# Moving the operands of one decoder block's matmuls to other byte offsets modulo 128

## The chip, the cores and the metric

The kernel runs on one NeuronCore of one Trainium2 chip. The metric is the time of one execution in device microseconds (us). The kernel before took 1974.78 us, the median of two runs (1974.39 and 1975.16).

## The reference

The reference is one hybrid decoder block for 256 tokens of width 2048, in float32. `proj = h @ w_in`, with `h` the rms-normalised input, gives the queries, keys, values and gates of two token mixers; both outputs are gated, merged and projected, and a gated feed-forward layer of width 5632 follows:

```
h = _rms_norm(x, attn_norm[l]);  proj = h @ w_in[l]
o_a = _nsa_mixer(...)            # compressed + selected + windowed attention
o_b = _gdn_mixer(...)            # short convolution, gated delta rule in chunks
mix = sigmoid(m_a) * (o_a @ w_branch_a[l]) + sigmoid(m_b) * (o_b @ w_branch_b[l])
x = x + mix @ w_out[l]
h2 = _rms_norm(x, ffn_norm[l])
x = x + (silu(h2 @ w_gate[l]) * (h2 @ w_up[l])) @ w_down[l]
```

Nearly all of the arithmetic is in the products with the large weight matrices, which are read once each from device memory.

## The kernel before

Every float32 number that enters a large product is split in two parts of the type fp32r, `hi` and `lo`, and a product is three matmuls: hi by hi, hi by lo and lo by hi. The matmul instruction of TensorE has a stationary operand (`lhsT`, 128 columns, which a weight load brings into the array ahead of the matmul) and a moving operand (`rhs`, which is streamed through it). In this kernel every matmul has a weight load of its own, also where the same stationary tile is used twice in a row.

`load_pair` (line 99) brings two k-tiles of a weight matrix, 128 rows by 512 columns each, into the tile `raw` by one DMA from the SP queue. ScalarE writes `whi` from it (line 107) and VectorE writes `wlo` (line 108). Both are tiles of two rows of 512 numbers to a partition, row j for k-tile j, and have three buffers each.

`chunk_tok` (line 113) makes 512 columns of a product for both tiles of 128 tokens: for each k-tile and each of the two token tiles three matmuls (lines 122 to 124), with a weight piece of 512 columns as the moving operand and a 128 by 128 piece of a transposed activation as the stationary one. `chunk_feat` (line 130) makes the same product transposed, for the convolved q, k and v of the gated delta rule: there a 128 by 128 piece of the weights is stationary and the activation, 256 tokens, is moving (lines 141 to 143).

The activations lie in tiles `hi` and `lo` with 16 k-tiles of 256 numbers to a partition. `big_tile` (line 93) takes them from a pool of four buffers of 16384 bytes, one behind the other. In the order of the program these tiles are the stationary operands of `chunk_tok`:

- `hT` (the normalised input), for `w_in`: the attention's projections, the output gates of the delta rule and the merge gates, 2112 matmuls. The same tiles are the moving operand of `chunk_feat`, 2304 matmuls.
- `oTA` and `oTB` (the outputs of the two mixers), for `w_branch_a` and `w_branch_b`, 384 matmuls each.
- `mixT`, for `w_out`, 384 matmuls.
- `h2T`, for `w_gate` and `w_up`, 2112 matmuls.
- `act`, for `w_down`, 1056 matmuls in four chunks. Its 44 k-tiles are split over three pairs of tiles: `act00` and `act10` (hi and lo of k-tiles 0 to 15, from the pool of four), `act01` and `act11` (16 to 31) and `act02` and `act12` (32 to 43), these four from another pool.

The address of a tile within a partition is fixed when the program is built. In the built program of the kernel before, `raw`, `whi`, `wlo` and every buffer of the pool of four start at 96 bytes modulo 128, and `act01`, `act11`, `act02` and `act12` start at 0. A k-tile takes 1024 bytes, a token tile 512, a row of `whi` or `wlo` 2048, so every piece that a matmul reads starts where its tile does, modulo 128.

The smaller work of the two mixers runs as side tasks between the pieces of the chunks (`run` and `pump`, lines 163 and 150): normalisations, transposes and small matmuls. A scheduler sets the final order on each engine when the program is built.

Of the kernel before, what the change touches and what calls it, by code (L numbers as in the profile page):

```python
# [9 lines left out]
F32 = mybir.dt.float32  # L10
F32R = mybir.dt.float32r
# [5 lines left out]
P = 128  # L17
S = 256
NT = 2
D = 2048  # L20
KD = D // P
# [22 lines left out]
def tile_hybrid_block(  # L44
# [22 lines left out]
    nc = tc.nc  # L67
    x = x[0]
# [11 lines left out]
    stream = ctx.enter_context(tc.tile_pool(name="stream", bufs=4))  # L80
    big = ctx.enter_context(tc.tile_pool(name="big", bufs=4))
# [1 line left out]
    psm = ctx.enter_context(tc.tile_pool(name="psm", bufs=4, space=bass.MemoryType.PSUM))  # L83
    pss = ctx.enter_context(tc.tile_pool(name="pss", bufs=4, space=bass.MemoryType.PSUM))

# [1 line left out]
    uid = [0]  # L87

    def nm(s):
        uid[0] += 1  # L90
        return f"{s}_{uid[0]}"

    def big_tile(name, dt=F32):
        return big.tile([P, KD, S], dt, tag="big", name=nm(name))

    def sps():
        return pss.tile([P, 512], F32, tag="sd", name=nm("sd"))
# [1 line left out]
    def load_pair(w, k0, c0, width):  # L99
        raw = stream.tile([P, 2, 512], F32, tag="raw", name=nm("raw"))  # L100
        nc.sync.dma_start(
            raw[:, :, :width],
            w[k0 * P : (k0 + 2) * P, c0 : c0 + width].rearrange("(k p) c -> p k c", p=P),
        )
        hi = stream.tile([P, 2, 512], F32R, tag="whi", name=nm("whi"), bufs=3)
        lo = stream.tile([P, 2, 512], F32R, tag="wlo", name=nm("wlo"), bufs=3)
        nc.scalar.activation(hi[:, :, :width], raw[:, :, :width], AF.Copy)  # L107
        nc.vector.tensor_tensor(  # L108
            lo[:, :, :width], raw[:, :, :width], hi[:, :, :width].bitcast(F32), ALU.subtract
        )  # L110
        return hi, lo

    def chunk_tok(w, c0, width, kts, stat, evac):
        ps = [psm.tile([P, 512], F32, tag="mm", name=nm("mm")) for _ in range(NT)]
        for k0 in range(0, kts, 2):
            hi, lo = load_pair(w, k0, c0, width)
            for j in range(2):
                kt = k0 + j
                for t in range(NT):
                    sh, sl = stat(kt, t)  # L120
                    o = ps[t][:, :width]
                    nc.tensor.matmul(o, lhsT=sh, rhs=hi[:, j, :width], start=kt == 0, stop=False)  # L122
                    nc.tensor.matmul(o, lhsT=sh, rhs=lo[:, j, :width], start=False, stop=False)  # L123
                    nc.tensor.matmul(o, lhsT=sl, rhs=hi[:, j, :width], start=False, stop=kt == kts - 1)  # L124
            yield
        for t in range(NT):
            evac(t, ps[t])
        yield
# [19 lines left out]
    side = deque()  # L148
# [16 lines left out]
            pump(n)  # L165

    def run_pair(ga, gb, n):
        """two chunks of which the last four k-tiles wait for the side tasks"""
        for g in (ga, gb):
            for _ in range(6):  # L170
                next(g)
                pump(n)
        drain()
# [3 lines left out]
        nc.vector.tensor_tensor(dst_lo, src, dst_hi.bitcast(F32), ALU.subtract)  # L177

    def transpose_hilo(src4, hi, lo, k0, t):
        """src4: four [P, P] pieces of a token-major tile, to k-tiles k0..k0+3 of hi and lo."""  # L180
        pt = sps()
        for i, s4 in enumerate(src4):
            nc.tensor.transpose(pt[:, i * P : (i + 1) * P], s4, ident)  # L183
        pv = pt.rearrange("p (k c) -> p k c", k=4)
        ts = slice(t * P, (t + 1) * P)
        hilo(hi[:, k0 : k0 + 4, ts], lo[:, k0 : k0 + 4, ts], pv)

# [1 line left out]
    ident = consts.tile([P, P], F32, name="ident")  # L189
    make_identity(nc, ident)  # L190
    identb = consts.tile([P, P], BF16, name="identb")
# [37 lines left out]
        nc.vector.tensor_copy(dst, pt[:, :n])  # L229
        return dst  # L230

# [1 line left out]
    scr = tc.tile_pool(name="nsa", bufs=1)  # L233
    nsa = scr.__enter__()
    hT_hi = big_tile("hT_hi", F32R)
    hT_lo = big_tile("hT_lo", F32R)
    xin = big.tile([P, NT, D], F32, tag="big", name="xin")
    for t in range(NT):
        for c in range(2):
            cs = slice(c * 1024, (c + 1) * 1024)  # L240
# [41 lines left out]
        ts = slice(t * P, (t + 1) * P)  # L282
        return hT_hi[:, kt, ts], hT_lo[:, kt, ts]

# [1 line left out]
    gates = consts.tile([P, NT, 48], F32, name="gates")  # L286
    beta = consts.tile([P, NT, H], F32, name="beta")
    gdec = consts.tile([P, NT, H], F32, name="gdec")
# [4 lines left out]
    def narrow():  # L293
# [5 lines left out]
        for k0 in range(0, KD, 8):  # L299
# [4 lines left out]
            for j in range(8):  # L304
                kt = k0 + j
                o = ps[:80, :S]
# [13 lines left out]
        nc.scalar.activation(beta, pv[:, :, 16:32], AF.Sigmoid)  # L320
        yield
        nc.vector.tensor_tensor(gdec, pv[:, :, 0:16], dtb.unsqueeze(1).to_broadcast([P, NT, H]), ALU.add)
        # softplus(a) = max(a, 0) + log1p(exp(-|a|)), the log1p as 2 artanh(e / (2 + e))
        e = consts.tile([P, NT, H], F32, name="sp_e")
        d = consts.tile([P, NT, H], F32, name="sp_d")
        s2 = consts.tile([P, NT, H], F32, name="sp_s2")
# [3 lines left out]
        nc.vector.reciprocal(d, d)  # L330
        nc.vector.tensor_tensor(e, e, d, ALU.mult)
        nc.vector.tensor_tensor(s2, e, e, ALU.mult)
        # the argument is at most 1/3, so terms to s^15 reach float32
        nc.vector.tensor_scalar(d, s2, 1.0 / 15, 1.0 / 13, ALU.mult, ALU.add)
        for q in (11, 9, 7, 5, 3):
            nc.vector.tensor_tensor(d, d, s2, ALU.mult)
# [20 lines left out]
        nc.sync.dma_start(grow_d, grow)  # L357
        yield

# [1 line left out]
    oTA_hi = big_tile("oTA_hi", F32R)  # L361
    oTA_lo = big_tile("oTA_lo", F32R)

# [21 lines left out]
        nc.vector.scalar_tensor_tensor(lo, src, gcol, hi.bitcast(F32), ALU.mult, ALU.subtract)  # L385

    def normed_T(pst, hi, lo, gcol):
        """rms-norm of four heads side by side, transposed, times a gain by channel"""
        sq = nsa.tile([P, 512], F32, tag="sq", name=nm("sq"), bufs=1)
        nc.scalar.activation(sq, pst, AF.Square)  # L390
        ss = nsa.tile([P, 4], F32, tag="ss", name=nm("ss"), bufs=4)
        nc.vector.tensor_reduce(ss, sq.rearrange("p (g d) -> p g d", g=4), AX.X, ALU.add)
        rs = nsa.tile([P, 4], F32, tag="rs", name=nm("rs"), bufs=4)
        rstd_of(ss, 1.0 / DH, EPS, rs)
        nv = nsa.tile([P, 512], F32, tag="nv", name=nm("nv"), bufs=2)
        nc.vector.tensor_tensor(
            nv.rearrange("p (g d) -> p g d", g=4),
            pst.rearrange("p (g d) -> p g d", g=4),
            rs.unsqueeze(2).to_broadcast([P, 4, P]),
            ALU.mult,  # L400
        )
        pt = sps()
        for i in range(4):
            nc.tensor.transpose(pt[:, i * P : (i + 1) * P], nv[:, i * P : (i + 1) * P], ident)
        gained(hi, lo, pt.rearrange("p (g d) -> p g d", g=4), gcol)
# [89 lines left out]
        return f  # L495

    def win_pair(pw):
        """columns 0:128 and 144:272 of a piece 272 wide, as [P, 2, 128]"""
        return bass.AP(tensor=pw.tensor, offset=pw.offset, ap=[list(pw.ap[0]), [144, 2], [1, 128]])

    def attend(gi, t, qh, ql):
# [93 lines left out]
    for gi in range(4):  # L595
        run(chunk_tok(w_in, C_Q + gi * 512, 512, KD, stat_h, evac_q(gi)), 1)

    # merge-gate logits and the product of branch A wait in DRAM for the merge
    keep = {n: dram.tile([NT, P, D], F32, name=n, bufs=1) for n in ("mA_d", "mB_d", "brA_d")}

    def evac_keep(n, c):
# [24 lines left out]
    for g in br:  # L626
        run(g)

# [1 line left out]
    oTB_hi = big_tile("oTB_hi", F32R)  # L630
    oTB_lo = big_tile("oTB_lo", F32R)
    scr = tc.tile_pool(name="gdn", bufs=1)
# [10 lines left out]
        return cw[r // 96][:, r % 96 : r % 96 + 1]  # L643

    def conv_silu(st, ps, base, silu_out):
        """short causal convolution of four heads by channel, then silu"""
        ca = gdn.tile([P, 4, S], F32, tag="ca", name=nm("ca"), bufs=2)
        for s in range(4):
            src = ps[s // 2][:, (s % 2) * S : (s % 2 + 1) * S]
            a = ca[:, s, :]  # L650
            nc.scalar.activation(a, src, AF.Copy, scale=conv_col(3, base + s))
            for i in (2, 1, 0):
                sh = 3 - i
                nc.vector.scalar_tensor_tensor(
                    a[:, sh:], src[:, : S - sh], conv_col(i, base + s), a[:, sh:], ALU.mult, ALU.add
                )
        silu_out(ca)
# [16 lines left out]
    nc.gpsimd.memset(p1, 0.0)  # L674
    p2 = gdn.tile([P, 8, 64], F32, name="p2")
    nc.gpsimd.memset(p2, 0.0)
    # one-hot columns for the blocks' inverses: lane = 32 * column group + problem
    unit = gdn.tile([P, 8, 32], F32, name="unit")
    nc.gpsimd.memset(unit, 0.0)
    uf = unit.rearrange("p c i -> p (c i)")  # L680
    for cg in range(4):
        for c in range(8):
            o = c * 32 + 8 * cg + c
            nc.gpsimd.memset(uf[cg * 32 : cg * 32 + 32, o : o + 1], 1.0)

    def gdn_prep(st, hg):
        """what hangs on the decay alone"""
        hs = slice(hg * 4, hg * 4 + 4)
        st.N = gdn.tile([P, 8, P], F32, tag="N", name=nm("N"), bufs=2)
        st.Q = gdn.tile([P, 8, P], F32, tag="Q", name=nm("Q"), bufs=2)  # L690
# [12 lines left out]
        for t in range(NT):  # L703
            for h in range(4):
                i = t * 4 + h
# [34 lines left out]
    def gdn_q(st, hg):  # L740
# [3 lines left out]
        for t in range(NT):  # L744
            for h0 in (0, 2):
                pk = sps()
                for h in (h0, h0 + 1):
                    nc.tensor.matmul(  # L748
                        pk[:, (h - h0) * 256 : (h - h0 + 1) * 256],
                        lhsT=st.kq[:, h, t, 0, :],  # L750
# [9 lines left out]
                    )  # L760
                    nc.vector.tensor_tensor(st.Q[:, i, :], pk[:, o + P : o + 2 * P], st.Q[:, i, :], ALU.mult)
                yield
        # the 32 x 32 blocks on the diagonal, a problem and eight of its columns to a lane
        ld = dram.tile([32, 32, 32], F32, tag="ld", name=nm("ld"))
        for b in range(4):
            bs = slice(32 * b, 32 * b + 32)
# [206 lines left out]
    for c in (2, 3):  # L973
        chunk_m("mB_d", c, 2)

# [1 line left out]
    mixT_hi = big_tile("mixT_hi", F32R)  # L977
    mixT_lo = big_tile("mixT_lo", F32R)

# [46 lines left out]
    for c in range(4):  # L1026
        run(chunk_tok(w_out, c * 512, 512, KD, stat_of(mixT_hi, mixT_lo), evac_out(c)))

# [1 line left out]
    act = [[], []]  # L1030
    for q in range(2):
        for i in range(3):
            if i == 2:
                act[q].append(fin.tile([P, 12, S], F32R, name=f"act{q}{i}"))
            elif i == 1:
                act[q].append(fin.tile([P, 16, S], F32R, name=f"act{q}{i}"))
            else:
                act[q].append(big_tile(f"act{q}{i}", F32R))
    rs2 = fin.tile([P, NT], F32, name="rs2")
    sst = fin.tile([P, NT], F32, name="sst")  # L1040
    nc.vector.tensor_reduce(sst, ss2, AX.X, ALU.add)
# [74 lines left out]
```

## Time and profile before

| what | value |
|---|---|
| median of two runs | 1974.78 us (1974.39 to 1975.16) |
| span of the profiled execution, first to last instruction | 1971.1 us |
| TensorE matmuls, busy | 1946.4 us (99%), 10485 records |
| TensorE weight loads, busy | 1651.0 us (84%) |
| VectorE, ScalarE, GpSimd busy | 1155.0, 928.4, 54.1 us |
| DMA | 367.04 MB, mean 186 GB/s |

The median stands 3.7 us above the span of the profiled execution; that is what lies around the span. The busy time of TensorE cannot tell how fast it works: matmuls are pipelined, a matmul of 512 columns is recorded as about 390 ns long, and the next one starts long before its end. What counts is the spacing, from the start of one matmul to the start of the next. It is read from the starts in a timeline, or from a stretch's length and its number of matmuls.

### The profile page before, as it was taken

To read this page: it belongs to the slowest core of one execution; us is meant where nothing else is said; L and a number is where in the kernel's file an instruction comes from. 1 tells how busy PE (TensorE), PEld (TensorE's weight loads), DVE (VectorE), ACT (ScalarE), POOL (GpSimd) and SP (SyncE) were. 2 spreads that over 40 slices of the span, in tenths; PEclk is the share of its full clock that TensorE was granted. 3 is DMA by queue.
4 is the path that set the end of the run, shared out by engine and by line. 5 is a ranking of instruction groups with operands and counts; after the bars stand their busy time and mean duration, and the time that the engine had idled before them with its cause. 6 is when DMAs were issued, how large, how long until landed. Compare 5 with 4: busy or idle time off the path is not lost.

```text
span 1971.1 us, 27260 instructions
## 1 busy us (share of the span) xinstructions
PE 1946.4 (99%) x10485; PEld 1651.0 (84%) x10485; DVE 1155.0 (59%) x1715; ACT 928.4 (47%) x1377; POOL 54.1 (3%) x97
## 2 busy tenths in 40 slices
PE   8999999999999999999999999999999999999999
PEld 6878877876998998999987788888888888888887
DVE  5555766655468587687774665554455444544443
ACT  5434555555454554654543544444444444443333
POOL 0001000001000000100100000000000000000000
PEclk9999999999999999999999999999999999999999
DMA  8566545546767566566574965666666666656663
GB/s 231 170 183 193 161 129 162 170 149 200 217 173 203 169 178 198 158 193 166 153 200 157 333 201 183 191 192 183 191 191 186 191 191 191 191 185 201 201 202 130
DMA packets 207605, 367.04 MB, mean 186 GB/s; under 512 B 25473, under 2 KB 34546, under 8 KB 207090
## 3 DMA queue, kind: packets, MB, share of 16 engines
q1 hardware_dynamic: 207442, 365.28, 62.1%
q8 instruction: 82, 1.34, 0.3%
q14 instruction: 49, 0.40, 0.1%
q10 hardware_dynamic: 32, 0.01, 0.0%
HBM read 355.76 MB, written 9.45 MB: 185 GB/s over the span
## 4 chain that ended last, share of the span: by engine, by line
PE 96%; DMA 2%; DVE 1%; ACT 0%; SPq 0%; issue 0%; POOL 0%; ACTq 0%; POOLq 0%; DVEq 0%
PE mm L123 25%; PE mm L124 24%; PE mm L122 24%; PE mm L141 4%; PE mm L143 4%; PE mm L142 4%; PE sd L183 1%; PE sd L668 1%; PE sd L448 1%; PE sd L561 1%; DMA Q<-grow_d 1%; PE sd L748 1%; DMA raw<-in_w_branch_b_dram 1%; PE sd L567 1%; PE sd L568 0%; PE sd L267 0%
## 5 line engine op out<-in xcount | busy, mean ns | idle before, releaser
L108 DVE TENSOR_TENSOR wlo<-raw,whi 128x1024 fp32r<-128x1024 f32 x632 | 773.7, 1225 | 658.5 <-ACT whi L107 656.1
L107 ACT ACTIVATE whi<-raw 128x1024 fp32r<-128x1024 f32 x632 | 669.7, 1060 | 804.5 <-PE mm L124 674.4
L123 PE MATMUL mm<-wlo,hT_hi 128*128 128x512 f32 x704 | 276.7, 393 | 0.0
L124 PE MATMUL mm<-whi,hT_lo 128*128 128x512 f32 x704 | 276.5, 393 | 0.0
L124 PE MATMUL mm<-whi,h2T_lo 128*128 128x512 f32 x704 | 274.0, 389 | 0.0
L123 PE MATMUL mm<-wlo,h2T_hi 128*128 128x512 f32 x704 | 273.9, 389 | 0.0
L122 PE MATMUL mm<-whi,hT_hi 128*128 128x512 f32 x704 | 260.2, 393 | 0.0
L122 PE MATMUL mm<-whi,h2T_hi 128*128 128x512 f32 x704 | 249.9, 390 | 0.0
L143 PE MATMUL mm<-hT_hi,wlo 128*128 128x256 f32 x768 | 218.4, 285 | 0.0
L141 PE MATMUL mm<-hT_hi,whi 128*128 128x256 f32 x768 | 218.4, 285 | 0.0
L142 PE MATMUL mm<-hT_lo,whi 128*128 128x256 f32 x768 | 218.3, 284 | 0.0
L124 PEld LDWEIGHTS mm<-whi,hT_lo 128*128 128x128 f32 x704 | 132.3, 188 | 27.7 <-issue 1.1
L123 PEld LDWEIGHTS mm<-wlo,hT_hi 128*128 128x128 f32 x704 | 132.3, 188 | 27.5 <-issue 1.1
L124 PEld LDWEIGHTS mm<-whi,h2T_lo 128*128 128x128 f32 x704 | 132.2, 188 | 27.5
L122 PEld LDWEIGHTS mm<-whi,h2T_hi 128*128 128x128 f32 x704 | 132.2, 188 | 27.1
L123 PEld LDWEIGHTS mm<-wlo,h2T_hi 128*128 128x128 f32 x704 | 132.2, 188 | 27.0
L122 PEld LDWEIGHTS mm<-whi,hT_hi 128*128 128x128 f32 x704 | 132.1, 188 | 26.3 <-issue 0.2
L141 PEld LDWEIGHTS mm<-hT_hi,whi 128*128 128x128 f32 x768 | 147.2, 192 | 0.6
L142 PEld LDWEIGHTS mm<-hT_lo,whi 128*128 128x128 f32 x768 | 147.2, 192 | 0.2
L143 PEld LDWEIGHTS mm<-hT_hi,wlo 128*128 128x128 f32 x768 | 146.9, 192 | 0.4
L123 PE MATMUL mm<-wlo,act 128*128 128x512 f32 x352 | 138.5, 393 | 0.0
L124 PE MATMUL mm<-whi,act 128*128 128x512 f32 x352 | 138.4, 393 | 0.0
(288 smaller groups left out, 2247.7 us busy)
## 6 DMA issues: line engine op xcount, KB each, us to landing
raw<-in_w_in_dram SPq DMA_DIRECT2D x272, 512.0 KB, 3.7
raw<-in_w_gate_dram SPq DMA_DIRECT2D x88, 512.0 KB, 4.4
raw<-in_w_up_dram SPq DMA_DIRECT2D x88, 512.0 KB, 3.7
raw<-in_w_down_dram SPq DMA_DIRECT2D x88, 512.0 KB, 4.7
raw<-in_w_branch_a_dram SPq DMA_DIRECT2D x32, 512.0 KB, 4.7
raw<-in_w_branch_b_dram SPq DMA_DIRECT2D x32, 512.0 KB, 4.9
raw<-in_w_out_dram SPq DMA_DIRECT2D x32, 512.0 KB, 4.7
wc<-in_w_cmp_dram SPq DMA_DIRECT2D x16, 256.0 KB, 4.2
```

The costliest lines, as they stand in the source:

```text
L107: nc.scalar.activation(hi[:, :, :width], raw[:, :, :width], AF.Copy)
L108: nc.vector.tensor_tensor(lo[:, :, :width], raw[:, :, :width], hi[:, :, :width].bitcast(F32), ALU.subtract)
L122: nc.tensor.matmul(o, lhsT=sh, rhs=hi[:, j, :width], start=kt == 0, stop=False)
L123: nc.tensor.matmul(o, lhsT=sh, rhs=lo[:, j, :width], start=False, stop=False)
L124: nc.tensor.matmul(o, lhsT=sl, rhs=hi[:, j, :width], start=False, stop=kt == kts - 1)
L141: nc.tensor.matmul(o, lhsT=hi[:, j, ws], rhs=xh[:, kt, :], start=first, stop=False, skip_group_check=True)
L142: nc.tensor.matmul(o, lhsT=hi[:, j, ws], rhs=xl[:, kt, :], start=False, stop=False, skip_group_check=True)
L143: nc.tensor.matmul(o, lhsT=lo[:, j, ws], rhs=xh[:, kt, :], start=False, stop=last, skip_group_check=True)
L183: nc.tensor.transpose(pt[:, i * P : (i + 1) * P], s4, ident)
L448: nc.tensor.matmul(pc[:60, :P], lhsT=kp[:, l0 + l, :], rhs=wc[:, l, :], start=l0 + l == 0, stop=l0 + l == 31)
L561: nc.tensor.transpose(pt[:n, r * P : (r + 1) * P], pb[:, r, c0 : c0 + n], ident)
L567: nc.tensor.matmul(po, lhsT=wh, rhs=ph[:n], start=i == 0, stop=False)
```

## The change

It moves tiles by a few bytes and leaves the work as it is. The built programs, before and changed, hold the same instructions in the same order on every engine; what differs is the addresses, and that ScalarE and VectorE write `whi` as two rows of 512 with a gap between them instead of 1024 numbers on end.

- `big_tile` and `xin` take 8 numbers (32 bytes) more, so the four buffers of the pool start at 96, 0, 32 and 64 modulo 128.
- `whi` gets 8 numbers between its two rows, so row 0 starts at 96 and row 1 at 0. `wlo` stays at 96 in both rows. To tell the rows apart, the three matmuls of `chunk_tok` stand twice in the source, for j = 0 and j = 1.
- The four later `act` tiles get 32 numbers more and start at chosen offsets inside. The act tiles have new names: `actAa` and `actAb` are hi and lo of the first 16 k-tiles, `actBa` and `actBb` of the next 16, `actCa` and `actCb` of the last 12.

Offsets modulo 128 of what a matmul reads, before and changed (`whi` is 96 before, and 96 in row 0 and 0 in row 1 changed; `wlo` is 96 in both):

| activation | hi before, changed | lo before, changed |
|---|---|---|
| hT | 96, 64 | 96, 32 |
| oTA, oTB | 96, 0 | 96, 96 |
| mixT | 96, 64 | 96, 32 |
| h2T | 96, 0 | 96, 96 |
| act, k-tiles 0 to 15 | 96, 64 | 96, 32 |
| act, k-tiles 16 to 31 | 0, 112 | 0, 16 |
| act, k-tiles 32 to 43 | 0, 96 | 0, 80 |

The diff, without comments that were removed:

```diff
     def big_tile(name, dt=F32):
-        return big.tile([P, KD, S], dt, tag="big", name=nm(name))
+        b = big.tile([P, KD * S + 8], dt, tag="big", name=nm(name))
+        return b[:, : KD * S].rearrange("p (k s) -> p k s", k=KD)
...
-        hi = stream.tile([P, 2, 512], F32R, tag="whi", name=nm("whi"), bufs=3)
+        hi = stream.tile([P, 2, 528], F32R, tag="whi", name=nm("whi"), bufs=3)
+        hi = hi.rearrange("p j c -> p (j c)")[:, :1040].rearrange("p (j c) -> p j c", j=2)[:, :, :512]
...
-                    nc.tensor.matmul(o, lhsT=sh, rhs=hi[:, j, :width], start=kt == 0, stop=False)
-                    nc.tensor.matmul(o, lhsT=sh, rhs=lo[:, j, :width], start=False, stop=False)
-                    nc.tensor.matmul(o, lhsT=sl, rhs=hi[:, j, :width], start=False, stop=kt == kts - 1)
+                    if j == 0:
+                        nc.tensor.matmul(o, lhsT=sh, rhs=hi[:, 0, :width], start=kt == 0, stop=False)
+                        nc.tensor.matmul(o, lhsT=sh, rhs=lo[:, 0, :width], start=False, stop=False)
+                        nc.tensor.matmul(o, lhsT=sl, rhs=hi[:, 0, :width], start=False, stop=False)
+                    else:
+                        nc.tensor.matmul(o, lhsT=sh, rhs=hi[:, 1, :width], start=False, stop=False)
+                        nc.tensor.matmul(o, lhsT=sh, rhs=lo[:, 1, :width], start=False, stop=False)
+                        nc.tensor.matmul(o, lhsT=sl, rhs=hi[:, 1, :width], start=False, stop=kt == kts - 1)
...
-    xin = big.tile([P, NT, D], F32, tag="big", name="xin")
+    xin = big.tile([P, KD * S + 8], F32, tag="big", name="xin")[:, : NT * D].rearrange("p (t d) -> p t d", t=NT)
...
+    OFF = ((28, 24), (4, 20))
     act = [[], []]
     for q in range(2):
         for i in range(3):
-            if i == 2:
-                act[q].append(fin.tile([P, 12, S], F32R, name=f"act{q}{i}"))
-            elif i == 1:
-                act[q].append(fin.tile([P, 16, S], F32R, name=f"act{q}{i}"))
+            if i > 0:
+                n = (16, 12)[i - 1]
+                a = fin.tile([P, n * S + 32], F32R, name=("actB", "actC")[i - 1] + "ab"[q])
+                off = OFF[q][i - 1]
+                act[q].append(a[:, off : off + n * S].rearrange("p (k s) -> p k s", k=n))
             else:
-                act[q].append(big_tile(f"act{q}{i}", F32R))
+                act[q].append(big_tile("actA" + "ab"[q], F32R))
```

## Rows read from the trace of the kernel before

**Rows 1.** The page: engines' busy time, share and records; the chain by engine.

```profile
PE 1946.4 (99%) x10485; PEld 1651.0 (84%) x10485; DVE 1155.0 (59%) x1715; ACT 928.4 (47%) x1377; POOL 54.1 (3%) x97
...
PE 96%; DMA 2%; DVE 1%; ACT 0%; SPq 0%; issue 0%; POOL 0%; ACTq 0%; POOLq 0%; DVEq 0%
```

**Rows 2.** Windows of TensorE: stretch, length, busy (records under way), clock, DMA.

```profile
518.80:555.10 36.30, 36.30 (x305) 1.00 0.71 198
592.90:636.40 43.50, 43.50 (x194) 1.00 0.69 198
1327.50:1371.00 43.50, 43.50 (x194) 1.00 0.63 185
1844.60:1866.30 21.70, 21.70 (x97) 1.00 0.69 217
1866.40:1888.70 22.30, 22.30 (x97) 1.00 0.58 189
1888.80:1905.50 16.70, 16.70 (x73) 1.00 0.61 187
```

**Rows 3.** Timeline of TensorE, h2T: start, us, engine, line, out<-moving,stationary.

```profile
1500.07 0.39 PE L123 MATMUL mm<-wlo,h2T_hi 128*128 128x512 f32 x1
...
1502.79 0.39 PE L123 MATMUL mm<-wlo,h2T_hi 128*128 128x512 f32 x1
```

**Rows 4.** Timeline of TensorE, act, k-tiles 16 to 31.

```profile
1867.98 0.40 PE L123 MATMUL mm<-wlo,act 128*128 128x512 f32 x1
1868.21 0.40 PE L124 MATMUL mm<-whi,act 128*128 128x512 f32 x1
1868.45 0.40 PE L122 MATMUL mm<-whi,act 128*128 128x512 f32 x1
...
1870.08 0.40 PE L123 MATMUL mm<-wlo,act 128*128 128x512 f32 x1
```

**Rows 5.** Timeline of TensorE, hT, behind a pause.

```profile
174.64 0.40 PE L124 MATMUL mm<-whi,hT_lo 128*128 128x512 f32 x1
174.87 0.40 PE L122 MATMUL mm<-whi,hT_hi 128*128 128x512 f32 x1
175.11 0.39 PE L123 MATMUL mm<-wlo,hT_hi 128*128 128x512 f32 x1
175.33 0.39 PE L124 MATMUL mm<-whi,hT_lo 128*128 128x512 f32 x1
175.56 0.40 PE L122 MATMUL mm<-whi,hT_hi 128*128 128x512 f32 x1
...
176.72 0.39 PE L124 MATMUL mm<-whi,hT_lo 128*128 128x512 f32 x1
```

**Rows 6.** Timeline of TensorE, the feature stage, behind a pause.

```profile
585.09 0.28 PE L142 MATMUL mm<-hT_lo,whi 128*128 128x256 f32 x1
...
586.16 0.28 PE L142 MATMUL mm<-hT_lo,whi 128*128 128x256 f32 x1
```

**Rows 7.** The chain in order of time: start, us, engine, line, records.

```profile
579.26 3.46 PE sd L748 x16
```

**Rows 8.** Groups by line: instruction, shape, count, busy and mean ns, idle before.

```profile
L108 DVE TENSOR_TENSOR wlo<-raw,whi 128x1024 fp32r<-128x1024 f32 x632 | 773.7, 1225 | 658.5 <-ACT whi L107 656.1
L107 ACT ACTIVATE whi<-raw 128x1024 fp32r<-128x1024 f32 x632 | 669.7, 1060 | 804.5 <-PE mm L124 674.4 <-PE mm L142 73.3 <-issue 31.1
```

**Rows 9.** Waits of TensorE for the split weights: total us, times, longest.

```profile
PE mm L123 <- DVE wlo L108: 3.3, 4, 1.7
PE mm L122 <- ACT whi L107: 1.0, 2, 0.7
```

## The prediction

> **What bounds the kernel now.** I read the page first: engines and chain [rows 1]. The reader is to see that matmuls are busy for 99% of the span and make up 96% of the chain of work that ended last. The other engines are busy for 59% and less. Only the speed of TensorE can move this time, and the engine is never short of work, so I looked for the spacing of its matmuls, from start to start.
>
> The windows give it by stage [rows 2]. Each of the six stretches holds large matmuls alone, and a window also counts the records under way when it opens: two of 512 columns (390 ns long, started some 227 ns apart), two or three of 256. So the first row says 36.30 us over 302 or 303 matmuls of 256 columns, 120 ns each; the second and third 43.50 us over 192 of 512 columns, 226.6 ns; the fourth, with `act` of k-tiles 0 to 15, 21.70 us over 95 or 96, 226 to 228. The last two, `act` of the later k-tiles, give 22.30 us over 95 or 96 and 16.70 us over 71 or 72: 232 to 235. [...]
>
> The timelines make it sharper. With `h2T` stationary, 12 spacings take 1502.79 - 1500.07 = 2.72 us, 226.7 ns each [rows 3]. With `act` of k-tiles 16 to 31, 9 spacings take 2.10 us, 233.3 each [rows 4]. The instructions are the same, and so are the moving tiles, which start at 96 modulo 128 in both. The stationary tiles start at 96 in the first case and at 0 in the second. That is the only trace of an offset's cost in this kernel: equal offsets 226.7, unequal ones 6.6 ns more.
>
> **The change, part by part.** No instruction is added, taken away or moved, on any engine or queue. What can change is how long each takes.
>
> *Writing whi in two rows.* ScalarE takes 1060 ns for a `whi`, VectorE 1225 ns for a `wlo` [rows 8]. One of each serves 12 matmuls, 12 x 226.7 = 2720 ns, or 24 of 256 columns, 24 x 120 = 2880 ns. So each engine works less than half of the time that it has, three buffers lie between, and TensorE waited 4.3 us in all for these two lines [rows 9]. I put this at nothing; the cover is gone only if one of them took over twice as long. Should matmuls become faster, the weights must come faster too: 193 GB/s at 226.7 ns (524288 bytes in 2.72 us) would be 202 at 216 ns, and the fourth window moved 217 [rows 2].
>
> *Matmuls whose weight load lies at another offset.* A weight load runs while the matmul before it streams, so the pair that counts is a matmul's moving piece and the next stationary one. The price of an unequal pair at the new distances stands in no row, so I bound it. Above: 233.3 ns, the settled spacing at the one unequal distance in this trace [rows 4]. Below: 216 ns, the shortest spacing at which records with a 128-column load before each follow one another here, the float32 products of line 748, 3.46 us over 16 [rows 7]. Between the two lies what equal offsets do behind a pause, when the load and the stream are not yet in step: 9 spacings in 176.72 - 174.64 = 2.08 us, 231.1 ns each, some 0.22 and some 0.24 us long, before they settle at 226.7 [rows 5]. I read these as samples of many relative positions of load and stream, and take 231 for an unequal pair, nearest to the settled unequal row and 4.4 above the equal one.
>
> - `hT`, `mixT` and `act` of k-tiles 0 to 15 (hi at 64, lo at 32, against 96 and 0): every pair is unequal. 2112 + 384 + 384 = 2880 matmuls x 4.4 ns = 12.7 us.
> - `h2T`, `oTA`, `oTB` (hi at 0, lo at 96): only row 0 of `whi` with hi is unequal, one pair in three, and these stand close together, in the six matmuls of row 0; the six of row 1 are equal. Since nine matmuls behind a pause are still unsettled [rows 5], six do not suffice to fall back into step. Ends: one third of 2880 (4.2 us) and all (12.7 us); I take two thirds, 8.4 us.
> - The later `act`, 672 matmuls: unequal before and nearly all unequal after, 233.3 to 231: -1.5 us.
> - The feature stage, 2304 matmuls of 256 columns: all unequal now (moving 64 and 32, stationary 96 and 0). Behind a pause 9 spacings there take 586.16 - 585.09 = 1.07 us, 118.9 each [rows 6], below the settled 120. So unequal offsets may give 1 ns back (-2.5 us) or cost what they do elsewhere (4.4 ns, +10.1 us); I take 0.
>
> Sum: 12.7 + 8.4 - 1.5 + 0 = +19.6 us. The profiled span of 1971.1 becomes 1990.7, and with the 3.7 us that the median stands above the span the time is **1994 us**, 1% more.
>
> [...]
>
> **The rivals.**
>
> *Faster: equal offsets are what costs.* Load and stream start in the same place of every 128 bytes and stay in each other's way; a well-chosen distance frees the stream. For it: 226.7 stands 10.7 above the 216 of line 748, where the load costs nothing to see, so there is something to win. Against it: the one unequal stretch is the slower one, and all through the unsettled rows no spacing falls below 0.22 us. Price at 216: 2880 x 10.7 = 30.8, a third of 2880 x 10.7 = 10.3, 672 x 17.3 = 11.6, and 2304 x 10.7 = 24.7 in the feature stage, 77 us: 1897 us. If half of the pairs gain, 1936. It decides where the new stages settle below 226 ns.
>
> *Slower by over 2%: every unequal pair costs what act shows.* Its place is the reading of the stationary piece beside the stream, in all stages that were equal. Price: 2880 x 6.6 = 19.0; the same 19.0 for `h2T` and `oT`, if the unequal third keeps the rest out of step; 2304 x 6.6 = 15.2 in the feature stage: 53 us, 2028 us. For it: this is the only settled row with unequal offsets. Against it: it shows one distance out of many, and six distances are in use now. The point from which it decides is 39.5 us over these 8064 matmuls, 4.9 ns on the mean.
>
> *No effect: the change does not do what it says.* The later `act` tiles also lie elsewhere in the partition, behind the pool of four; it may be their place and not their offset that costs 6.6 ns. Then nothing moves: 1975 us. Against it: the other tiles lie far apart too, and all of those run at 226.7.
>
> **How the numbers follow.** Forecast 0.50, with its own range from 1980 (229 ns for an unequal pair, a third in `h2T`) to 2009 (all of `h2T`, and 10 us in the feature stage); no effect 0.12; slower 0.20; faster 0.18, of which the milder third stays within 2%. A change within 2%, 1935 to 2014 us, is about what a measurement cannot tell from none. Hence faster 0.13, within 2% 0.67, slower 0.20. The range runs from 1940, near the halved gain, to 2026, just short of the full loss; some 0.13 is left out below and 0.07 above.
>
> **What would show it right or wrong.** The busy shares will hardly move, so the spacing by stage decides, from windows of pure stretches or the timeline. Right: `hT`, `mixT` and the first `act` stretch at 229 to 233 ns, `h2T` between 228 and 231 and not settling at 226.7, later `act` slightly below 233, the feature stage at 119 to 122. Faster: some stage settles at 216 to 224. Slower: 233 and more in all of them, and a feature stage at 125 or above. No effect: 226.7 everywhere but in the later `act`, still 233. The two rows of `whi` now have lines of their own, so within one stage the spacings behind row 0 and row 1 must differ if the pair sets the price, and a `wlo` matmul with `h2T` lo, both at 96, should be the one nearest to 226.7. Wrong in another way: a wait for `whi` or `wlo` of more than a few us, which would mean that writing two rows costs time.

## The result: 1% slower, with two misses that cancel

The changed kernel takes 1993.43 us, the median of two runs (1992.97 and 1993.89), against 1974.78 before: 1.0091 times as long, with a 95% interval of 1.0062 to 1.0121. The forecast was 1994. The profiled execution has a span of 1992.2 us, 21.1 more than before, at a granted clock of 0.997 (0.998 before). The medians differ by 18.7 us only. In every run with both numbers, 1.7 or 1.8 us lie around the span; of the 3.7 us that I put there for the kernel before, some 2 us are therefore not that, but a profiled execution that was faster than the median.

The page of the changed kernel, engines and chain, answers to [rows 1]:

```profile
PE 1967.3 (99%) x10485; PEld 1648.4 (83%) x10485; DVE 1155.9 (58%) x1715; ACT 928.8 (47%) x1377; POOL 55.3 (3%) x97
...
PE 97%; DMA 2%; DVE 1%; ACT 0%; SPq 0%; issue 0%; POOL 0%; ACTq 0%; DVEq 0%; POOLq 0%
```

The same 10485 matmul records are busy for 20.9 us longer, and no other engine's row of the page moved by more than 2.6 us. So nearly the whole difference lies in how fast matmuls follow one another. The page's groups for the two engines that write the weights, and the waits of TensorE for them, answer to [rows 8] and [rows 9]:

```profile
L110 DVE TENSOR_TENSOR wlo<-raw,whi 128x1024 fp32r<-128x1024 f32 x632 | 774.0, 1226 | 674.0 <-ACT whi L109 671.0
L109 ACT ACTIVATE whi<-raw 128x1024 fp32r<-128x1024 f32 x632 | 670.0, 1061 | 819.1 <-PE mm L131 696.2
```
```profile
PE mm L126 <- DVE wlo L110: 2.5, 2, 1.9
PE mm L125 <- ACT whi L109: 0.9, 2, 0.7
```

Writing `whi` in two rows takes 1 ns more than the 1060 before, and TensorE waits 3.4 us where it waited 4.3. The windows of stretches with large matmuls alone answer to [rows 2]: the feature stage, `hT`, `h2T`, and the second and third part of `act`.

```profile
525.70:561.40 35.70, 35.70 (x306) 1.00 0.71 200
729.30:773.70 44.40, 44.40 (x193) 1.00 0.69 201
1611.60:1656.00 44.40, 44.40 (x194) 1.00 0.63 183
1887.60:1909.70 22.10, 22.10 (x97) 1.00 0.60 192
1909.80:1926.40 16.60, 16.60 (x73) 1.00 0.56 186
```

The granted clock is 1.00 in all five, as in [rows 2], so the clock is not what differs. With the records under way taken off (two or three of 256 columns, two of 512 in the long stretches, one or two in the short ones), these are 118 ns for 256 columns, and 232, 231, 230 to 233 and 231 to 234 for 512. The later `act` was 232 to 235 before, so it gained a little, which the sums below make sharper; the feature stage gained as well. The timeline of `h2T` answers to [rows 3]. Its lines 125 to 127 are the matmuls of the first k-tile of a pair, 129 to 131 those of the second:

```profile
1652.15 0.40 PE L126 MATMUL mm<-wlo,h2T_hi 128*128 128x512 f32 x1
1652.39 0.40 PE L127 MATMUL mm<-whi,h2T_lo 128*128 128x512 f32 x1
1652.62 0.40 PE L129 MATMUL mm<-whi,h2T_hi 128*128 128x512 f32 x1
...
1655.19 0.40 PE L127 MATMUL mm<-whi,h2T_lo 128*128 128x512 f32 x1
```

From the first to the last row are 13 spacings (one record among them stands for two matmuls), 3.04 us: 233.8 ns each, a little above the stage's mean of 232.0. Before, they were an even 226.7.

Summed from start to start over all neighbouring large matmuls of a stage, the traces give, in us:

| stage | before | changed | difference | forecast |
|---|---|---|---|---|
| hT, mixT, first act | 641.2 | 652.7 | +11.5 | +12.7 |
| h2T, oTA, oTB | 657.9 | 672.1 | +14.1 | +8.4 |
| later act | 156.5 | 155.6 | -0.9 | -1.5 |
| feature stage | 274.6 | 269.8 | -4.8 | 0 |
| sum | | | +19.9 | +19.6 |

### The profile page after: what moved, and what is told of

It is laid out like the page before. It is cut to its first block, busy times and chain, and to the rows that moved or that the text cites. A ratio compares the mean times of both kernels' runs of the same rounds, so it can differ in the third digit from the quotient of the medians.

```text
span 1992.2 us, 27260 instructions
## 1 busy us (share of the span) xinstructions
PE 1967.3 (99%) x10485; PEld 1648.4 (83%) x10485; DVE 1155.9 (58%) x1715; ACT 928.8 (47%) x1377; POOL 55.3 (3%) x97
## 4 chain that ended last, share of the span: by engine, by line
PE 97%; DMA 2%; DVE 1%; ACT 0%; SPq 0%; issue 0%; POOL 0%; ACTq 0%; DVEq 0%; POOLq 0%
PE mm L126 12%; PE mm L129 12%; PE mm L127 12%; PE mm L130 12%; PE mm L131 12%; PE mm L125 12%; PE mm L150 4%; PE mm L148 4%; PE mm L149 4%; PE sd L190 1%; PE sd L675 1%; PE sd L455 1%; PE sd L568 1%; PE sd L755 1%; PE sd L574 0%; PE sd L575 0%
## 5 line engine op out<-in xcount | busy, mean ns | idle before, releaser
L131 PEld LDWEIGHTS mm<-whi,hT_lo 128*128 128x128 f32 x352 | 66.2, 188 | 16.2 <-issue 0.8
L127 PEld LDWEIGHTS mm<-whi,h2T_lo 128*128 128x128 f32 x352 | 66.0, 188 | 16.2
```

The source lines that it names most:

```text
L127: nc.tensor.matmul(o, lhsT=sl, rhs=hi[:, 0, :width], start=False, stop=False)
L131: nc.tensor.matmul(o, lhsT=sl, rhs=hi[:, 1, :width], start=False, stop=kt == kts - 1)
```

## The experiments

In every experiment the matmuls are those of the kernel before, in number and, but for e8, in shape; what is meant to differ is the addresses alone. In e1 `whi` is also written as two rows, in e5 and e7 to e12 one or two small tiles share buffers, to make room, and in e9 to e12 this shifts the order of some small instructions. All use one edit, by which a table `MOVE` gives the numbers (of 4 bytes) by which hi and lo of an activation are moved in their buffers; the `act` tiles outside the pool take their entries in the same way. It is shown as in e2, e3, e4 and e6; the room of 32 numbers (128 bytes) is 64 in e10 and nothing in the others:

```diff
-    def big_tile(name, dt=F32):
-        return big.tile([P, KD, S], dt, tag="big", name=nm(name))
+    def big_tile(name, dt=F32, off=0):
+        b = big.tile([P, KD * S + 32], dt, tag="big", name=nm(name))
+        return b[:, off : off + KD * S].rearrange("p (k s) -> p k s", k=KD)
```

The table has the mean spacing in ns of every stage, worked out from the starts of neighbouring large matmuls (pauses, over 243 ns for 512 columns and over 137 for 256, left out; the unsettled matmuls behind them are in, which lifts `hT` and `oTA` by a ns where the stage is even). "Act 1, 2, 3" are its three parts. Times are single executions, but medians of five for e5, e9, e11 and e12; the kernel before ran beside them on the same chips, 1974.8 for e1 to e4 and between 1973.2 and 1978.9 for the others.

| run | hT | mixT | h2T | oTA | act 1, 2, 3 | feature | us |
|---|---|---|---|---|---|---|---|
| before | 227.7 | 226.9 | 226.8 | 228.0 | 226.9, 233.3, 233.3 | 119.9 | 1974.8 |
| changed | 231.6 | 231.7 | 232.0 | 231.9 | 231.2, 231.7, 231.8 | 117.7 | 1993.4 |
| e1 | 231.8 | 231.8 | 231.8 | 231.8 | 231.7, 231.9, 232.5 | 118.4 | 1995.6 |
| e2 | 232.0 | 232.2 | 231.7 | 231.8 | 232.2, 231.2, 227.3 | 117.9 | 1992.8 |
| e3 | 233.0 | 233.2 | 232.8 | 231.8 | 233.3, 233.3, 233.3 | 117.2 | 2001.2 |
| e4 | 233.3 | 233.3 | 230.6 | 231.0 | 233.3, 232.0, 226.8 | 118.3 | 1995.0 |
| e5 | 231.0 | 230.9 | 230.8 | 231.1 | 230.9, 231.0, 231.0 | 118.6 | 1992.0 |
| e6 | 233.0 | 233.1 | 233.3 | 233.3 | 233.1, 233.3, 233.3 | 121.8 | 2011.8 |
| e7 | 231.0 | 230.8 | 230.8 | 231.0 | 230.9, 231.1, 231.0 | 114.0 | 1982.6 |
| e8 | 231.0 | 230.9 | 230.8 | 231.0 | 230.9, 230.3, 231.4 | 118.3 | 1989.5 |
| e9 | 227.7 | 226.9 | 226.8 | 228.1 | 226.7, 226.7, 226.7 | 116.3 | 1964.5 |
| e10 | 232.4 | 232.3 | 231.2 | 231.3 | 233.0, 233.3, 232.3 | 119.2 | 1998.5 |
| e11 | 227.8 | 226.9 | 226.8 | 227.8 | 226.7, 226.7, 226.7 | 117.8 | 1966.2 |
| e12 | 227.8 | 226.9 | 226.8 | 227.5 | 226.7, 226.7, 226.7 | 113.8 | 1959.8 |

**e1, the rows of whi alone.** Only the second row of `whi` is moved by 32 bytes; the activations stay.

```diff
-        hi = stream.tile([P, 2, 512], F32R, tag="whi", name=nm("whi"), bufs=3)
+        hi = stream.tile([P, 2, 528], F32R, tag="whi", name=nm("whi"), bufs=3)
+        hi = hi.rearrange("p j c -> p (j c)")[:, : 2 * 520].rearrange("p (j c) -> p j c", j=2)[:, :, :512]
```

> Only whi's row 1 moves, to 0 modulo 128; all stationary activations stay at 96 (later act at 0). Pair theory (the distance between a moving piece and the next stationary one sets the price of each matmul alone): in h2T the two thirds of the row-1 matmuls whose moving piece is whi cost about 231 ns, all others 226.7, mean 228; time about 1984 us. Step theory (a stage settles at a fixed spacing only if offsets repeat from matmul to matmul; alternating offsets keep it unsettled): every pair, the equal ones too, means 231 to 232; time 1992 to 1998 us.

It took 1995.6 us, 20.8 more than before: this edit alone costs as much as the whole change. It does more than move a row, though; see e5.

**e2, the activations alone.** `whi` and `wlo` stay at 96; the activations have the changed kernel's offsets modulo 128.

```diff
+        "hT": (24, 16), "mixT": (24, 16), "actA": (24, 16),
+        "oTA": (8, 0), "oTB": (8, 0), "h2T": (8, 0), "actB": (28, 4), "actC": (24, 20),
```

> Only the stationary tiles move, to the offsets of the changed kernel (hi and lo differ); whi and wlo stay at 96 in both rows. Pair theory: in h2T wlo with lo (equal) at 226.7, the other two of three at about 232, mean 230; time about 1993 us. Step theory: no stage settles, all pairs mean 231 to 232, time 1992 to 1998 us.

1992.8 us, 18.0 more. So the two parts do not add up: either one takes the stages out of their even spacing (all but the last part of `act`, at 227.3), and the other then changes little.

**e3 and e4, one distance to a stage.** Hi and lo of a stage lie at one offset modulo 128, another one in each stage.

```diff
+        # e3
+        "hT": (24, 24), "mixT": (24, 24), "actA": (24, 24),
+        "oTA": (16, 16), "oTB": (16, 16), "h2T": (16, 16), "actB": (20, 20), "actC": (28, 28),
+        # e4
+        "hT": (8, 8), "mixT": (8, 8), "actA": (8, 8),
+        "oTA": (12, 12), "oTB": (12, 12), "h2T": (12, 12), "actB": (12, 12), "actC": (24, 24),
```

> One distance (stationary minus moving) in each stage, the same for hi and lo and both rows: 96 in hT, mixT and the first act, 64 in h2T and oT, 112 in act of k-tiles 16 to 31, 16 in the last act; feature stage 32. Pair theory: every stage at the unequal price, 231 to 233 ns, feature stage 118 to 122. Step theory: each stage settles after some ten matmuls in a short repeating pattern with a mean of its own between 224 and 236 ns; some distance may lie below 226.7.

> One distance in each stage again: 32 in hT, mixT and the first act, 48 in h2T and oT, 80 in act of k-tiles 16 to 31, 0 in the last act; feature stage 96. Pair theory: 231 to 233 ns but in the last act, 226.7. Step theory: each stage settles in a pattern of its own; hT at 32 repeats 233.3, as the later act tiles did before, and the last act, at equal offsets in the tile that cost 233.3, goes to 226.7. If it is the place of the later act tiles that costs, the last act stays at 233.3 and hT at 226.7.

2001.2 and 1995.0 us. Of the stages of 512 columns in the table, the thirteen with unequal offsets lie between 230.6 and 233.3, none below. The last part of `act` in e4 has its offsets equal to those of the weights, in the place where it ran at 233.3 before, and there it runs at 226.8. Its timeline:

```profile
1914.78 0.39 PE L137 MATMUL mm<-whi,actCb 128*128 128x512 f32 x1
...
1917.28 0.39 PE L136 MATMUL mm<-wlo,actCa 128*128 128x512 f32 x1
```

These are 11 spacings (one record between stands for two matmuls) in 2.50 us, 227 each. And `hT`, in the pool of four where it ran at 227.7, runs at 233.3 with its offset 32 bytes on. It is the offset, not the place.

**e5, all equal modulo 128.** The later `act` tiles come to 96 modulo 128 as well. The buffers of `whi` and `wlo` get 32 numbers of room, of which the feature stage uses 8 to put its distance at 32.

```diff
-        hi = stream.tile([P, 2, 512], F32R, tag="whi", name=nm("whi"), bufs=3)
+        hi = stream.tile([P, 1056], F32R, tag="whi", name=nm("whi"), bufs=3)
+        hi = hi[:, off : off + 1024].rearrange("p (j c) -> p j c", j=2)
...
+        "actB": (24, 24), "actC": (24, 24),
```

> A version that should beat both. All stationary activations of the 512-column stages and both weight tiles at 96 (distance 0 everywhere, the later act tiles too); only in the feature stage the weight tiles start 32 bytes later (distance 32). If what the runs so far showed holds by stage: 226.8 ns in every 512-column stage (672 matmuls of the later act gain 6.5 ns each, 4.4 us), feature stage 117.2 instead of 119.9 (2304 x 2.7 = 6.2 us): 1964 us against 1974.8. Rival (pair prices from before alone, feature stage not helped): 1970.

1991.98 us against 1975.9 beside it, a ratio of 1.0083 (1.0069 to 1.0097). Every stage of 512 columns is at 231, though all its offsets are equal modulo 128. The built program shows what I had overlooked: a weight buffer of 1056 numbers is 4224 bytes, 16 and a half times 256, so the three buffers of `whi` lie at 96, 224 and 96 modulo 256. The timeline of `h2T`:

```profile
1659.64 0.39 PE L138 MATMUL mm<-wlo,h2T_hi 128*128 128x512 f32 x1
...
1662.18 0.40 PE L137 MATMUL mm<-whi,h2T_hi 128*128 128x512 f32 x1
```

11 spacings (one record stands for two) in 2.54 us: 230.9 each. The title's "modulo 128" is half of what counts. In e1 and in the changed kernel `whi` has such a buffer too, and in e2 to e4 and e6 the pool of four has one (16512 bytes). So e1 does not tell the moved row from the buffers' 128 bytes, which by themselves give 231.0 here against e1's 231.8. And in the pool of four, hi and lo of e3, e4 and e6 lie 128 bytes apart modulo 256; one distance to a stage have only the second and third part of `act`, at 112 and 16 modulo 256 in e3, 80 and 0 in e4, 124 and 248 in e6.

**e6, a few bytes.** Modulo 128, distances of 4 and 8 bytes in the pool of four, 124 and 120 in the later `act`. Modulo 256, two thirds of the pairs in the pool of four are 132 and 136 apart; the last part of `act` is 8 bytes short of equal in every pair.

```diff
+        "hT": (1, 1), "mixT": (1, 1), "actA": (1, 1),
+        "oTA": (2, 2), "oTB": (2, 2), "h2T": (2, 2), "actB": (23, 23), "actC": (22, 22),
```

> Distances of a few bytes, one to a stage: 4 in hT, mixT and the first act, 8 in h2T and oT, 124 in act of k-tiles 16 to 31, 120 in the last act, 124 in the feature stage. If the price follows the exact byte distance, each stage has a level of its own unlike 226.8, 225 to 235; if only blocks of 16 or 32 bytes count, 4 and 8 behave as 0 (226.8) and 124 and 120 as 112 (233.3).

2011.8 us, the slowest of all, about 36 above the kernel before: 233.0 to 233.4 in all stages of 512 columns, and 121.8 in the feature stage, the only run that is slower there than before. The last part of `act`:

```profile
1990.27 0.40 PE L136 MATMUL mm<-wlo,actCa 128*128 128x512 f32 x1
...
1992.37 0.40 PE L136 MATMUL mm<-wlo,actCa 128*128 128x512 f32 x1
```

9 spacings (one record between stands for two matmuls) in 2.10 us, 233.3 each: 8 bytes are enough for the level of [rows 4].

**e7, another base.** As e5, with every tile 32 bytes further on, and the feature stage's weights moved by 64 bytes.

```diff
+    base = consts.tile([P, 8], F32, name="base")
+    nc.vector.memset(base, 0.0)
...
-            hi, lo = load_pair(w, k0, c0, 512)
+            hi, lo = load_pair(w, k0, c0, 512, 16)
```

> All tiles 32 bytes further on, moving and stationary at 0 modulo 128, distance 0; feature stage at distance 64. If only the distance counts, 226.8 in every 512-column stage, as at 96; if the offset itself counts, another level. Feature stage: between 116 and 118.

The stages of 512 columns repeat e5 to 0.2 ns: they do not notice a shift of everything by 32 bytes. That speaks for distances and against absolute offsets; other shifts, and a shift of the even state, were not run. The feature stage fell to 114.0, the surprise of this run, and the time to 1982.6 us. There the distances modulo 256 alternate between 64 and 192.

**e8, shorter weight loads.** The offsets of e5 in the 512-column stages, and the loads of the second and third part of `act` cut to 64 and 32 columns. It leaves out the products for the other tokens there.

```diff
-                    o = ps[t][:, :width]
+                    m = P if kts == KD or kt < 16 or kt == kts - 1 else 64 if kt < 32 else 32
+                    sh, sl, o = sh[:, :m], sl[:, :m], ps[t][:m, :width]
```

> Later act tiles at distance 0, and there the stationary pieces are cut to 64 columns (k-tiles 16 to 31) and 32 columns (32 to 42), so those products are left out for the other tokens; the moving pieces stay 512 columns. If the 10.7 ns above 216 come from the weight load being read beside the stream, they shrink with its columns: about 221 and 218 to 219 ns. If they are a fixed price of changing the stationary operand, both stay at 226.7. Feature stage at distance 16: 117 to 120.

230.3 and 231.4 ns, against 231.0 for whole loads in e5: half or a quarter of the columns changes next to nothing. But with these buffers the stages are not in their even state, so what a short load does to 226.7 was not measured. Inconclusive for that.

**e9, equal modulo 256.** Weight buffers of 4352 bytes, 17 times 256, and later `act` tiles that start at the weights' 96 modulo 256 (by a tile of 64 numbers ahead of them instead of 8). The feature stage's weights are moved by 64 bytes.

```diff
-        hi = stream.tile([P, 2, 512], F32R, tag="whi", name=nm("whi"), bufs=3)
+        hi = stream.tile([P, 1088], F32R, tag="whi", name=nm("whi"), bufs=3)
+        hi = hi[:, off : off + 1024].rearrange("p (j c) -> p j c", j=2)
...
-    ss2 = fin.tile([P, NT, 4], F32, name="ss2")
+    ss2 = fin.tile([P, 64], F32, name="ss2")[:, :8].rearrange("p (t c) -> p t c", t=NT)
```

> A version that should beat both: moving and stationary pieces at equal offsets modulo 256 in every 512-column stage (buffers of whi and wlo 4352 bytes apart, so modulo 512 they alternate by 256), later act tiles included; in the feature stage the weight pieces lie 64 bytes further on. If what has to repeat is the offset modulo 256, every 512-column stage settles at 226.8 and the feature stage at 114: 1974.8 - 4.4 (672 x 6.5 ns) - 13.6 (2304 x 5.9 ns) = 1957 us. If it has to repeat modulo 512, the 512-column stages stay at 231 as in the version with equal offsets modulo 128, and the time is about 1982 us.

1964.47 us against 1974.99 beside it, 0.9948 (0.9934 to 0.9962). All stages of 512 columns are at the even spacing, the later `act` too, and the three buffers alternate modulo 512. So equal offsets modulo 256 suffice (226.7 to 228.1 here), modulo 128 they do not (230.8 to 231.1 in e5). The feature stage, with 64 throughout, came to 116.3 and not to the 114.0 of e7, and so the time missed the 1957 that I expected.

**e10, half a turn.** Distances of 128, 64 and 192, and hi at 0, lo at 128 in `h2T`, `oTA` and `oTB`.

```diff
+        "hT": (32, 32), "mixT": (32, 32), "actA": (32, 32),
+        "oTA": (0, 32), "oTB": (0, 32), "h2T": (0, 32), "actB": (16, 16), "actC": (48, 48),
```

> Distances modulo 256 that modulo 128 are 0: 128 throughout in hT, mixT and the first act; 0 for hi and 128 for lo in h2T and oT; 64 in act of k-tiles 16 to 31 and 192 in the last act; feature stage 128. Whi and wlo as before. If a repeating pattern is what settles, hT gets one fixed spacing of its own (226.8, if only the distance modulo 128 counts; another level, if 256 does) and h2T, where hi and lo differ, does not settle and means 230 to 232. If the pair prices the matmul, h2T is a mixture of 226.8 and the level of hT, two thirds to one. Feature stage 114 to 120.

1998.5 us. Distances of 128, 64 and 192 throughout a stage give 232 to 233, the mixed stages 231. The groups of TensorE by line in `h2T`, where a record is the longer, the later the next matmul starts (389 or 390 at the 226.8 of the stage before, 392 to 397 at the 232.0 of the changed one):

```profile
L136 PE MATMUL mm<-whi,h2T_lo 128*128 128x512 f32 x704 | 279.4, 397 | 0.0
L135 PE MATMUL mm<-wlo,h2T_hi 128*128 128x512 f32 x704 | 278.7, 396 | 0.0
...
L134 PE MATMUL mm<-whi,h2T_hi 128*128 128x512 f32 x704 | 250.1, 391 | 0.0
```

A pair is again a matmul's moving piece and the next stationary one. From start to start, line 135, which makes an unequal pair, takes 232.4 ns on the mean; line 136, an equal pair right after an unequal one, 234.0; line 134, an equal pair after an equal one, 227.0. So the same distance of 0 costs 227 or 234, by what stands before it. Nine in ten of these spacings come back, within 1 ns, with every 12 matmuls, the loop over two k-tiles and two token tiles; so they do in e6's `h2T`, with spacings of 226 to 239. In the changed kernel 85% come back after 36 matmuls, the three weight buffers, and only 34% after 12. So these mixed stages run in sequences that repeat with their addresses. That alone would also fit a price for each pair; the equal pairs at 227 and 234 do not.

**e11 and e12, the feature stage.** As e9, with the feature stage's weights moved by 192 bytes, and by 64 (`whi`) and 192 (`wlo`).

```diff
-            hi, lo = load_pair(w, k0, c0, 512)
+            hi, lo = load_pair(w, k0, c0, 512, (48, 48))    # e11
+            hi, lo = load_pair(w, k0, c0, 512, (16, 48))    # e12
```

> As the version with equal offsets modulo 256, but in the feature stage both weight tiles lie 192 bytes further on instead of 64. If the feature stage's level is set by the distance modulo 128, it stays at 116.3 and the time at 1964 us; if 192 was the better part of the mixture of 64 and 192 that ran at 114.0, it goes to 113.3 to 114 and the time to 1958 us.

> The same, but in the feature stage whi lies 64 and wlo 192 bytes further on. If it was the mixture of the two, 113.3 to 114 ns and 1958 us, and the version with 192 throughout stays at 116; if not, 116 to 118 ns and 1964 us or more. If any alternation costs, as in the 512-column stages, it is slower than both uniform versions.

The feature stage came to 117.8 ns with 192 throughout, 116.3 with 64 throughout (e9) and 113.8 with both: the mixture does it, as the second expectation had it. e11 took 1966.16 us (ratio 0.9954, 0.9942 to 0.9967), e12 1959.75 (0.9921, 0.9908 to 0.9935), with 1975.91 for the kernel before beside both. e12 is the fastest version found. Its page:

```profile
span 1955.8 us, 27261 instructions
...
PE 1930.8 (99%) x10485; PEld 1639.8 (84%) x10485; DVE 1153.8 (59%) x1715; ACT 928.1 (47%) x1377; POOL 54.2 (3%) x97
```

Its windows of the feature stage, `h2T` and the second part of `act`:

```profile
520.30:554.80 34.50, 34.50 (x306) 1.00 0.74 204
1627.70:1671.20 43.50, 43.50 (x194) 1.00 0.65 185
1853.30:1875.00 21.70, 21.70 (x97) 1.00 0.61 192
```

and its timeline in the feature stage and in the second part of `act`:

```profile
524.74 0.28 PE L155 MATMUL mm<-hT_hi,whi 128*128 128x256 f32 x1
...
525.99 0.28 PE L157 MATMUL mm<-hT_hi,wlo 128*128 128x256 f32 x1
```
```profile
1859.64 0.39 PE L137 MATMUL mm<-wlo,actBa 128*128 128x512 f32 x1
...
1862.36 0.39 PE L137 MATMUL mm<-wlo,actBa 128*128 128x512 f32 x1
```

11 spacings in 1.25 us are 113.6 ns; 12 spacings in 2.72 us (one record between stands for two) are 226.7, where [rows 4] had 233.3. Summed as above, the feature stage fell from 274.6 to 261.3 us and the later `act` from 156.5 to 152.1, 17.7 us together; the medians differ by 16.2.

## Why the total was right and the reason only in part

**Bound, and the split weights.** Right. TensorE's spacing makes up 19.9 of the 21.1 us between the two spans, and the rows of `whi` cost nothing that shows.

**The cost of unequal offsets.** 231 ns was taken from the rows behind a pause [rows 5]; `hT`, `mixT` and the first `act` now run at 231.6, 231.7 and 231.2. The term of 12.7 us came out as 11.5. That it fits so well is partly luck: unsettled equal offsets are not unequal ones, and at the offsets of e3, e4 and e6 the same stages run at 233. Of the bounds, 233.3 and 216, one was good: 233.3 is reached in e3, e4, e6 and e10, while nothing with 512 columns went below 226.7 on the mean. The 216 was misread: line 748's records have 256 columns of plain float32, not 512 of fp32r, and it was no shortest spacing, since the feature stage runs at 120.

**The step that failed: "the pair that counts is a matmul's moving piece and the next stationary one".** I took a third of `h2T`'s pairs as unequal and two thirds of the stage as paying. All of it pays: `h2T` runs at 232.0, above my 228 to 231, and the term is 14.1 us against 8.4, above even the upper end of 12.7 that I gave. That a load runs beside the matmul ahead of it does show; of the two matmuls in the first row, the second starts at 1499.84, as the load for the one at 1500.07 does:

```profile
1499.61 0.62 PE L122 MATMUL mm<-whi,h2T_hi 128*128 128x512 f32 x2
1500.07 0.39 PE L123 MATMUL mm<-wlo,h2T_hi 128*128 128x512 f32 x1
```
```profile
1499.84 0.19 PEld L123 LDWEIGHTS mm<-wlo,h2T_hi 128*128 128x128 f32 x1
```

Two things were wrong all the same. The first is the count: modulo 256, where the buffers of `whi` lie 128 bytes apart, 1155 of the 2089 pairs of `h2T` without a pause are unequal, more than half and not a third. The second is the rule itself, and the signs I had named settle it. The groups of TensorE by line (first `h2T` before, at a spacing of 226.8; then the changed kernel, at 232.0):

```profile
L124 PE MATMUL mm<-whi,h2T_lo 128*128 128x512 f32 x704 | 274.0, 389 | 0.0
L123 PE MATMUL mm<-wlo,h2T_hi 128*128 128x512 f32 x704 | 273.9, 389 | 0.0
...
L122 PE MATMUL mm<-whi,h2T_hi 128*128 128x512 f32 x704 | 249.9, 390 | 0.0
```
```profile
L129 PE MATMUL mm<-whi,h2T_hi 128*128 128x512 f32 x352 | 139.7, 397 | 0.0
...
L127 PE MATMUL mm<-whi,h2T_lo 128*128 128x512 f32 x352 | 139.0, 395 | 0.0
L130 PE MATMUL mm<-wlo,h2T_hi 128*128 128x512 f32 x352 | 138.9, 394 | 0.0
...
L131 PE MATMUL mm<-whi,h2T_lo 128*128 128x512 f32 x352 | 138.1, 392 | 0.0
L126 PE MATMUL mm<-wlo,h2T_hi 128*128 128x512 f32 x352 | 137.9, 392 | 0.0
...
L125 PE MATMUL mm<-whi,h2T_hi 128*128 128x512 f32 x352 | 114.1, 395 | 0.0
```

The mean over the first row (lines 125 to 127) is 394.0, over the second 394.3, where they should have differed; from start to start it is 232.1 and 231.9 ns. Line 129, from `whi` at 0 to hi at 0, is an equal pair modulo 128 and has the longest record of all; the pairs of `wlo` and lo, lines 126 and 130, at 392 and 394, are far from the 389 of the even stage. Counted modulo 256 the pairs fare no better: equal ones average 231.8 ns in the changed `h2T`, 231.3 in e5, 231.0 in e1, 230.5 in e10 and 230.1 in e2, but 226.8 where the whole stage is equal. Nor is the pair before enough: an equal pair after an equal one takes 227.0 in e10, but 231.3 in e5 and 234.3 in the changed kernel. So what a matmul costs in these runs depends on the sequence that it stands in. Not every unequal pair breaks the even state: in e2's last part of `act` a third of the pairs stand 240 bytes apart modulo 256, and the stage runs at 227.3.

**The feature stage.** I took 0, between -2.5 and +10.1; it gave 4.8 back. For these matmuls of 256 columns equal offsets are nearly the worst of the cases that were run, 119.9; only e6's distances, 124 and 252 modulo 256, are worse, 121.8. The rows behind a pause, 118.9 [rows 6], had the right sign. These 4.8 us hide the 5.7 by which the other term was too small; the total owes its accuracy to that.

**The rivals.** "Equal offsets are what costs" fell for 512 columns, at all the distances that were run, and held, in part, for 256: 274.6 to 261.3 us in e12, 13.3 of the 24.7 that I had priced. "Every unequal pair costs what act shows" is nearly e6, +36 us, so its level is real in the stages of 512 columns, but the offsets of this change are not the ones that reach it. "It may be their place" fell with e4 and again with e9, where the same tiles run at 226.7.

With other addresses the same 10485 matmuls take 36 us more than the kernel before in e6, and 10.5 us less in e9.

**What stays open** is the mechanism. The runs show that in the 512-column stages equal offsets modulo 256 of what is streamed and what is loaded go with an even 226.7 (e9) and equal ones modulo 128 alone with 231.0 (e5), that a mixed stage is not the sum of prices of its pairs (equal ones at 227.0 and 234.0 in e10), and that loads of 64 and 32 columns leave uneven stages at 230.3 and 231.4 (e8, 231.0 with whole loads in e5). None of them shows by what means the offsets act, or why the feature stage wants the opposite: it differs from the others in its columns and in having the weights as the stationary operand, and no run separates the two.

## What to carry to other kernels

Where TensorE is busy for 99% and every matmul has a weight load of its own, read the spacing from start to start by stage: two stages of the same shape at different spacings are the sign to look at the addresses. Here it paid to keep all buffers of streamed and loaded operands at one offset modulo 256 in the 512-column stages (226.7 in e9; weight buffers of 4224 bytes, an odd multiple of 128, broke it in e5 without any offset being written down, 231.0), and to set them apart by 64 and 192 bytes in the 256-column stage (113.8 in e12 against 119.9): 0.8% for no work (1959.75 us against 1975.91). A forecast that is right in sum should still be read term by term.

## What was not expected of the hardware

- Offsets equal modulo 128 do not give the even spacing, offsets equal modulo 256 do: 231.0 in e5 against 226.7 in e9.
- A few bytes were enough for the full 233.3 of [rows 4]: the last part of `act` ran at it with its tiles 8 bytes short of equal (e6).
- The feature stage and the stages of 512 columns want opposite things: with equal offsets 119.9 and 226.8; with a distance of 64, 116.3 (e9) and 233.3 (e10); with 192, 117.8 (e11) and 232.3 (e10). The feature stage is fastest with both at once, 113.8 (e12).
- The same spacings come back under other addresses: 226.7 of [rows 3] in the later `act` of e9, e11 and e12, 233.3 of [rows 4] in that of e3 and e6. No run shows what stands behind them.
